# Decay attention: the key bias as two rows of the second score product, the causal mask as an addend of the minimum

## The chip, the cores and the metric

The kernel runs on one core of one Trainium2 chip. The metric is the device time of one execution in microseconds (us), and the time of a kernel is the median of several runs. Beside the runs, one execution is taken by the hardware profiler; every duration that is quoted comes from such an execution.

The engines' names in the profile: PE is TensorE's matrix products, PEld its weight loads, DVE is VectorE, ACT is ScalarE, POOL is GpSimd and SP the engine that issues most loads. "L733" is line 733 of the kernel.

## The reference

The kernel computes one layer of a hybrid trunk on 1024 frames of 1024 features: a state-space branch and a forgetting-attention branch side by side, then cross-attention into 256 memory tokens, then a gated FFN. The change touches the forgetting attention alone, 8 heads of 64:

```python
def forgetting_attention(q, k, v, f_logit):
    scale = 1.0 / math.sqrt(hd)
    cum_log_f = jnp.cumsum(jax.nn.log_sigmoid(f_logit.astype(jnp.float32)), axis=1)
    ...
        s = jnp.einsum('bqhd,bkhd->bhqk', qb, kb).astype(jnp.float32) * scale
        bias = cum_log_f[:, :, q0:k_end, None] - cum_log_f[:, :, None, :k_end]
        ...
        s = jnp.where(mask, s + bias, NEG_INF)
        p = jax.nn.softmax(s, axis=-1)
        outs.append(jnp.einsum('bhqk,bkhd->bqhd', p.astype(v.dtype), vb))
```

A query sees the keys up to its own position. The bias has one part for the query and one for the key. The query's part is the same for all keys of a row, so the softmax does not see it, and the kernel uses the key's part only.

## The kernel before

**Number format.** The large products run in a rounded 32-bit format (F32R). Where full precision is wanted, an operand is split into a rounded high part and the low remainder: `split` (L112) has ACT copy the high part (L113) and VectorE subtract it (L115, or L117 with a factor). `mm3` (L121) is then three products: high x high, high x low, low x high (L122 to L124).

**Stages.** (1) The input projections, with the state-space branch's coefficients worked out on VectorE beside them. `qk_tile` (L284) makes a block of q or k, takes it out of PSUM on VectorE (L289), splits it (through L113 and L115) and has POOL's queue store both halves in `qk_d` (L297, L298). q is stored with the factor -0.125, so all that follows works with negated scores, and the softmax's maximum is a minimum. In the middle of this stage `f_gate` (L336) turns the gate's logits, takes the logarithm of the sigmoid and its running sum over the 1024 frames (L348) in a tile of 8 rows, one per head, and POOL's queue stores that in `nc_d` (L349). The state-space branch then ends on VectorE (L621 to L624); SP loads its matrix T (L632), and `ssm_out` multiplies with it (L643, L644). (2) The attention stage, `fox` (L705), with fillers beside it. (3) The output projection, cross-attention and FFN, nearly all of it products on PE.

**The attention stage.** `fox` goes through 64 units, a head h and a block t of 128 queries, head by head. For each unit there are three steps, and their instructions are offered in a pipeline: the scores of a unit come two units ahead of its turning.

- `prepare(h)` (L709), offered at block 1 of the head before, issues five loads on SP's queue: the head's row of `nc_d`, broadcast to all 128 rows (`ncb`, a tile of tag b, 2 buffers, L714); q's high rows above q's low rows (`qs`, tag a, L718); and into `ka` k's high and low rows, twice, in rows 0 to 63 and 64 to 127 (L720).
- `scores(h, t)` (L722) fills a PSUM tile `s` (two buffers) with (t + 1) x 128 columns, at most 512 in one product: first `qs` against k's high rows, then `qs` against k's low rows (L730, L731). So each product sums over 128 rows: 64 with q's high part and 64 with its low part. A third, bf16 product of the identity with `maskb` adds 1e30 to the diagonal block's keys that lie ahead of the query (L733). Then one VectorE operation adds `ncb`, writes the sums to the tile `c` and leaves each row's minimum (L737, with a second instruction that reads the accumulator). ACT takes the exponential with the minimum as its bias and sums it (L739), VectorE takes the reciprocal (L740) and scales (L741).
- `turn(h, t)` (L744) transposes the unit's blocks on PE (L758) and copies them out of PSUM on ACT or VectorE (L761, L763). After two units of two heads, `values` (L765) multiplies with v on halves of the array (L772, 64 columns each).

Fillers (L975) are offered beside this at a fixed rate (`paced`, L887): the second half of v (`v1`), the gated unit, the normalised memory (`mem_load`, VectorE's L959), the state-space half of the output projection, the memory's keys and values, and a product of weights for the cross-attention. They use the same four PSUM buffers `g`.

At the end of the stage the loads of stage 3 go into the buffers that the attention frees: t1 into tiles of tags a and b (L1039), the weights of the output projection (L1026).

**What sets the order.** The program is offered as written, but the order of the instructions on each engine is made by a planner: it simulates the kernel with its own costs, starts what is ready by priority, and gives buffers out as they come free. Each engine, and each queue of loads, then runs its list in that order, and an instruction that waits holds up what stands behind it on its engine.

Of the kernel before, what the change touches and what calls it, by code (L numbers as in the profile page):

```python
# [9 lines left out]
F32 = mybir.dt.float32  # L10
F32R = mybir.dt.float32r
BF16 = mybir.dt.bfloat16
AF = mybir.ActivationFunctionType
ALU = mybir.AluOpType
# [3 lines left out]
P = 128  # L18
S = 1024
# [5 lines left out]
NH = 8  # L25
# [27 lines left out]
def layer(ctx: ExitStack, tc: tile.TileContext, a, out):  # L53
# [30 lines left out]
    def sm(n, name):  # L84
        return small.tile([P, n], F32, name=name, tag=name)

    ident = const.tile([P, P], F32, name="ident")
    make_identity(nc, ident)
    identb = const.tile([P, P], BF16, name="identb")
    dve.tensor_copy(identb, ident)  # L90
    ones = const.tile([P, 1], F32, name="ones")
    dve.memset(ones, 1.0)
    epsc = const.tile([P, 2], F32, name="epsc")
    for i in range(2):
        dve.memset(epsc[:, i:i + 1], (EPS, 4 * EPS)[i])
    maskb = const.tile([P, P], BF16, name="maskb")
    pool.memset(maskb, 0.0)
    pool.affine_select(out=maskb, in_=maskb, pattern=[[-1, P]], compare_op=ALU.is_ge,
                       fill=-NEG, base=0, channel_multiplier=1)
    gains = const.tile([P, 5, KT], F32, name="gains")  # L100
    with tc.high_priority(offset=2 * 5000):
# [10 lines left out]
    def split(hi, lo, src, mul=None, lo_eng=None):  # L112
        first = act.activation(out=hi, in_=src, func=AF.Copy, scale=1.0 if mul is None else mul)  # L113
        if mul is None:
            (lo_eng or dve).tensor_tensor(out=lo, in0=src, in1=hi.bitcast(F32), op=ALU.subtract)  # L115
        else:
            dve.scalar_tensor_tensor(out=lo, in0=src, scalar=mul, in1=hi.bitcast(F32),  # L117
                                     op0=ALU.mult, op1=ALU.subtract)
        return first
# [29 lines left out]
    stA, stB, stC = pool, pool, pool  # L149
# [29 lines left out]
    v_d = dram.tile([NT, P, 512], F32, name="v_d")  # L179
    h_d = dram.tile([16, NG, HP + P], F32, name="h_d")  # L180
    T_d = dram.tile([2, P, 16 * P], F32, name="T_d")
    nc_d = dram.tile([NH, S], F32, name="nc_d")
    t1_d = dram.tile([L, NC, D], F32, name="t1_d")
    kv_d = dram.tile([16, P, 256], F32, name="kv_d")
    x1_d = dram.tile([NT, P, D], F32, name="x1_d")
# [9 lines left out]
    def tt(tag, shape=None, dt=F32):  # L195
        return t4.tile(shape or [P, S], dt, name=tag, tag=tag, bufs=BUFS[tag])

    def t2t(shape, dt=F32):
        return tt("t2", shape, dt)
# [136 lines left out]
    def f_gate(ftok):  # L336
        ps = s_ps([P, S])[0:NH]
        for j in range(NT):
            pe.transpose(ps[:, j * P:(j + 1) * P], ftok[:, j], ident)
        f, fl = ps, tt("a", [NH, S])  # L340
        dve.tensor_scalar(out=f, in0=ps, scalar1=fb, scalar2=None, op0=ALU.add)
        f = f.rearrange("p (j c) -> p c j", j=L)
        fc = fl.rearrange("p (c j) -> p c j", j=L)
        act.activation(out=fc, in_=f, func=AF.Abs)
        act.activation(out=fl, in_=fl, func=AF.Exp, scale=-1.0)
        act.activation(out=fl, in_=fl, func=AF.Ln, bias=1.0)
        dve.scalar_tensor_tensor(out=fc, in0=f, scalar=0.0, in1=fc, op0=ALU.min, op1=ALU.subtract)
        dve.tensor_tensor_scan(out=fl, data0=fl, data1=fl, initial=0.0, op0=ALU.add, op1=ALU.min)  # L348
        stA.dma_start(out=nc_d, in_=fl)  # L349


    def cmul(o_re, o_im, x_re, x_im, y_re, y_im, t):
# [352 lines left out]
    def fox(yf):  # L705
# [3 lines left out]
        def prepare(h):  # L709
            r0 = (h % 2) * 64  # L710
            qs = tt("a", [P, S], F32R)
            ka = slab([P, 2, S])
            ncb = tt("b")
            sp.dma_start(out=ncb, in_=nc_d[h:h + 1, :].broadcast_to([P, S]))  # L714
            heads[h] = (qs, ka, ncb)
            q, k = qs.bitcast(F32), ka.bitcast(F32)
            for t in range(2):
                sp.dma_start(out=q[t * 64:t * 64 + 64], in_=qk_d[h // 2, t, r0:r0 + 64])  # L718
            for rr in (0, 64):
                sp.dma_start(out=k[rr:rr + 64], in_=qk_d[4 + h // 2, :, r0:r0 + 64].rearrange("t p s -> p t s"))  # L720

        def scores(h, t):  # L722
            qs, ka, ncb = heads[h]
            ke = (t + 1) * P
            ps = s_ps([P, S])
            qt = qs[:, t * P:(t + 1) * P]
            for c0 in range(0, ke, 512):
                c1 = min(ke, c0 + 512)
                dg = c1 == ke
                pe.matmul(ps[:, c0:c1], qt, ka[:, 0, c0:c1], start=True, stop=False)  # L730
                pe.matmul(ps[:, c0:c1], qt, ka[:, 1, c0:c1], start=False, stop=not dg)  # L731
                if dg:
                    pe.matmul(ps[:, ke - P:ke], identb, maskb, start=False, stop=True)  # L733
            sc = tt("c")
            nlr = sm(3, "nlr")
            nm, l, rl = (nlr[:, i:i + 1] for i in range(3))
            dve.tensor_tensor_reduce(out=sc[:, :ke], in0=ps[:, :ke], in1=ncb[:, :ke], scale=1.0,  # L737
                                     scalar=3e38, op0=ALU.add, op1=ALU.min, accum_out=nm)
            last.append(act.activation(out=sc[:, :ke], in_=sc[:, :ke], func=AF.Exp, scale=-1.0, bias=nm, accum_out=l))  # L739
            dve.reciprocal(out=rl, in_=l)  # L740
            dve.tensor_scalar(out=sc[:, :ke], in0=sc[:, :ke], scalar1=rl, scalar2=None, op0=ALU.mult)  # L741
            units[h, t] = sc
# [873 lines left out]
```

## Time and profile before

| | us |
|---|---|
| median of 3 runs | 1416.56 |
| lowest and highest run | 1413.81, 1417.14 |
| the profiled execution | 1412.18 |
| its span, first to last instruction | 1410.4 |
| mean granted TensorE clock over the span | 0.990 |

| products on PE in the attention stage | number | mean of one, ns |
|---|---|---|
| score products of 512 columns, L730 and L731 | 48 and 48 | 449 and 405 |
| mask products, L733 | 64 | 233 |
| transpositions, L758 | 288 | 280 |
| value products of 256 columns, L772 | 256 | 395 |

How to read it: the span is what the profiler saw between the first and the last instruction; the execution's own time has a little around it. Products are pipelined, so one's duration is longer than the time until the next starts: what a product costs is read from the starts. "Granted clock" is the share of TensorE's full speed that it was allowed in a stretch.

### The profile page before, as it was taken

To read this page: it belongs to the slowest core of one execution; us is meant where nothing else is said; L and a number is where in the kernel's file an instruction comes from. 1 tells how busy PE (TensorE), PEld (TensorE's weight loads), DVE (VectorE), ACT (ScalarE), POOL (GpSimd) and SP (SyncE) were. 2 spreads that over 40 slices of the span, in tenths; PEclk is the share of its full clock that TensorE was granted. 3 is DMA by queue.
4 is the path that set the end of the run, shared out by engine and by line. 5 is a ranking of instruction groups with operands and counts; after the bars stand their busy time and mean duration, and the time that the engine had idled before them with its cause. 6 is when DMAs were issued, how large, how long until landed. Compare 5 with 4: busy or idle time off the path is not lost.

```text
span 1410.4 us, 20272 instructions
## 1 busy us (share of the span) xinstructions
PE 1381.5 (98%) x7353; PEld 1163.3 (82%) x7353; DVE 952.1 (68%) x1719; ACT 652.8 (46%) x1289; POOL 378.7 (27%) x430
## 2 busy tenths in 40 slices
PE   9999999999999898999999999999999999999997
PEld 7889888889888786888888788888888888888886
DVE  8949945857666687545467767777776676555566
ACT  7383345666566555433344532333333334544351
POOL 0011110011111133001021377676766651000021
PEclk9999999889999999999999999999999999999999
DMA  6335665357562855024467345554444447965544
GB/s 217 91 107 162 204 224 135 91 165 224 187 180 95 214 185 201 1 83 159 147 213 250 102 174 195 186 173 168 144 159 151 162 150 244 344 203 194 179 165 164
DMA packets 104502, 239.45 MB, mean 170 GB/s; under 512 B 11465, under 2 KB 40137, under 8 KB 104273
## 3 DMA queue, kind: packets, MB, share of 16 engines
q1 hardware_dynamic: 85872, 176.24, 39.8%
q0 software_dynamic: 18528, 61.91, 12.3%
q8 instruction: 58, 0.95, 0.3%
q14 instruction: 44, 0.35, 0.1%
HBM read 169.43 MB, written 77.33 MB: 175 GB/s over the span
## 4 chain that ended last, share of the span: by engine, by line
PE 60%; DVE 1%; ACT 0%; issue 0%; DVEq 0%; ACTq 0%
PE x L1281 17%; PE g L1281 13%; PE x L1544 7%; PE g L1544 7%; PE x L123 2%; PE x L124 2%; PE g L122 2%; PE x L122 2%; PE g L124 2%; PE g L123 2%; PE g L1066 1%; PE g L1177 1%; DVE c L1054 0%; DVE whl L115 0%; ACT yt L1048 0%
## 5 line engine op out<-in xcount | busy, mean ns | idle before, releaser
L1281 PE MATMUL x<-slab,op 128*128 128x512 f32 x984 | 233.2, 389 | 0.5 <-DVE op L115 0.5
L1281 PEld LDWEIGHTS x<-slab,op 128*128 128x128 f32 x984 | 184.7, 188 | 39.2 <-DVE op L115 1.0
L1281 PE MATMUL g<-slab,op 128*128 128x512 f32 x744 | 178.7, 389 | 0.0
L115 DVE TENSOR_TENSOR slab<-slab 128x1024 fp32r<-128x1024 f32 (+2 forms) x92 | 110.6, 1208 | 86.6 <-ACT slab L113 84.4
L1281 PEld LDWEIGHTS g<-slab,op 128*128 128x128 f32 x744 | 139.7, 188 | 29.0
L122 PE MATMUL g<-slab,whl 128*128 128x512 f32 (+1 forms) x416 | 151.7, 365 | 0.8 <-ACT slab L485 0.4
L124 PE MATMUL g<-slab,whl 128*128 128x512 f32 (+1 forms) x416 | 148.9, 359 | 0.0
L123 PE MATMUL g<-slab,whl 128*128 128x512 f32 (+1 forms) x416 | 148.3, 356 | 0.0
L113 ACT ACTIVATE slab<-slab 128x1024 fp32r<-128x1024 f32 (+2 forms) x92 | 94.9, 1036 | 107.9 <-DMA slab<-hs_d 79.0
L1544 PE MATMUL g<-slab 128*128 128x512 f32 x462 | 126.6, 389 | 0.0
L1544 PE MATMUL x<-slab 128*128 128x512 f32 x462 | 126.6, 389 | 0.0
L1544 PEld LDWEIGHTS g<-slab 128*128 128x128 f32 x462 | 86.7, 188 | 18.0
L1544 PEld LDWEIGHTS x<-slab 128*128 128x128 f32 x462 | 86.7, 188 | 18.0
L115 DVE TENSOR_TENSOR op<-slab,op 128x512 fp32r<-128x512 f32 x80 | 84.4, 1066 | 11.6 <-ACT op L113 11.3
L1357 POOL TENSOR_TENSOR wt<-wt 128x256 f32<-128x256 f32 x88 | 83.0, 943 | 21.3 <-DMA wt<-in_w_down 18.0
L122 PEld LDWEIGHTS g<-slab,whl 128*128 128x128 f32 x416 | 78.6, 189 | 12.0 <-ACT whl L113 0.6
L124 PEld LDWEIGHTS g<-slab,whl 128*128 128x128 f32 x416 | 78.4, 189 | 11.7 <-DVE whl L115 0.2
L122 PE MATMUL g<-whl,slab 128*128 128x256 f32 (+2 forms) x288 | 86.8, 310 | 1.2 <-ACT yt L318 0.7
L123 PEld LDWEIGHTS g<-slab,whl 128*128 128x128 f32 x416 | 78.6, 189 | 10.8
L113 ACT ACTIVATE op<-slab 128x512 fp32r<-128x512 f32 x80 | 50.0, 627 | 79.3 <-PE x L1281 38.0
L124 PE MATMUL g<-whl,slab 128*128 128x256 f32 (+2 forms) x288 | 85.9, 299 | 0.0
L123 PE MATMUL g<-whl,slab 128*128 128x256 f32 (+2 forms) x288 | 85.9, 298 | 0.0
(385 smaller groups left out, 2890.6 us busy)
## 6 DMA issues: line engine op xcount, KB each, us to landing
hs_d<-ev POOLq DMA_DIRECT2D x77, 256.0 KB, 2.6
slab<-hs_d SPq DMA_DIRECT2D x35, 512.0 KB
wt<-in_w_down SPq DMA_DIRECT2D x44, 256.0 KB
wt_d<-wt POOLq DMA_DIRECT2D x22, 512.0 KB, 5.1
slab<-in_w_gate SPq DMA_DIRECT2D x20, 512.0 KB
slab<-in_w_up SPq DMA_DIRECT2D x20, 512.0 KB
slab<-wt_d SPq DMA_DIRECT2D x20, 512.0 KB
wd_d<-in_w_down SPq DMA_DIRECT2D x33, 256.0 KB
```

What stands on the lines that cost most here:

```text
L113: first = act.activation(out=hi, in_=src, func=AF.Copy, scale=1.0 if mul is None else mul)
L115: (lo_eng or dve).tensor_tensor(out=lo, in0=src, in1=hi.bitcast(F32), op=ALU.subtract)
L122: pe.matmul(ps, lh, rh, start=first, stop=False)
L123: pe.matmul(ps, lh, rl, start=False, stop=False)
L124: pe.matmul(ps, ll, rh, start=False, stop=last)
L1066: pe.transpose(tp[:, k], src[:, (k0 + k) * P:(k0 + k + 1) * P], ident)
L1177: turned = pe.transpose(tp[:, k], h3[:, (4 * n + k) * P:(4 * n + k + 1) * P], ident)
L1281: pe.matmul(ps, x[:, k], y[:, k], start=first and k + n == 0, stop=k == 3 and n == 2, skip_group_check=not first)
L1357: pool.tensor_tensor(out=o, in0=x, in1=y, op=ALU.subtract)
L1544: pe.matmul(banks[n][j], xo[:, u, js], wo[:, v], start=ends[0] and k == 0, stop=ends[1] and k == 2, skip_group_check=onto is not None)
```

## The change

The key's bias leaves VectorE's addition and enters through the second score product. Its low-part sum is cut from 128 rows to 66: 64 rows of q's high part against k's low part, and two rows of ones (`one_d`) against the bias, split into a rounded high row and a low row. (q's low part against k's low part is no longer computed.) For that `f_gate` splits the running sum in two halves of 512 columns, stores a high and a low row per head, and fills and stores the rows of ones. `prepare` builds a second tile `q1` of 66 rows in place of `ncb`, and `ka` gets the bias in rows 64 and 65 of its low half.

VectorE's addition then has its second operand free, and it takes the mask: a constant of 512 columns, zero but for its last 128. The diagonal block is always the last 128 columns of a row, so the operation takes the constant's last columns. For blocks 4 to 7 the row is longer than 512, and the operation is made twice: on the first 512 columns, with one zero column repeated as the addend, and on the rest, starting from the first one's minimum (`low`). The product with the identity (L733) and the identity in bf16 go.

```diff
-    identb = const.tile([P, P], BF16, name="identb")
-    dve.tensor_copy(identb, ident)
...
-    maskb = const.tile([P, P], BF16, name="maskb")
+    maskb = const.tile([P, 512], BF16, name="maskb")
     pool.memset(maskb, 0.0)
-    pool.affine_select(out=maskb, in_=maskb, pattern=[[-1, P]], compare_op=ALU.is_ge,
+    pool.affine_select(out=maskb[:, 384:], in_=maskb[:, 384:], pattern=[[-1, P]], compare_op=ALU.is_ge,
                        fill=-NEG, base=0, channel_multiplier=1)
...
-    nc_d = dram.tile([NH, S], F32, name="nc_d")
+    nc_d = dram.tile([NH, 2, S], F32, name="nc_d")
+    one_d = dram.tile([2, S], F32, name="one_d")
...
         dve.tensor_tensor_scan(out=fl, data0=fl, data1=fl, initial=0.0, op0=ALU.add, op1=ALU.min)
-        stA.dma_start(out=nc_d, in_=fl)
+        for h in range(2):
+            hs = slice(h * 512, h * 512 + 512)
+            hi = t2t([NH, 512], F32R)
+            split(hi, fl.bitcast(F32R)[:, hs], fl[:, hs])
+            stA.dma_start(out=nc_d[:, 0, hs], in_=hi.bitcast(F32))
+        stA.dma_start(out=nc_d[:, 1], in_=fl)
+        one = tt("yt", [2, 256])
+        dve.memset(one, 1.0)
+        for i in range(4):
+            stA.dma_start(out=one_d[:, i * 256:i * 256 + 256], in_=one)
...
             ka = slab([P, 2, S])
-            ncb = tt("b")
-            sp.dma_start(out=ncb, in_=nc_d[h:h + 1, :].broadcast_to([P, S]))
-            heads[h] = (qs, ka, ncb)
-            q, k = qs.bitcast(F32), ka.bitcast(F32)
+            q1 = tt("b", [66, S], F32R)
+            heads[h] = (qs, q1, ka)
+            q, k, o = qs.bitcast(F32), ka.bitcast(F32), q1.bitcast(F32)
             for t in range(2):
                 sp.dma_start(out=q[t * 64:t * 64 + 64], in_=qk_d[h // 2, t, r0:r0 + 64])
-            for rr in (0, 64):
-                sp.dma_start(out=k[rr:rr + 64], in_=qk_d[4 + h // 2, :, r0:r0 + 64].rearrange("t p s -> p t s"))
+            sp.dma_start(out=k[0:64], in_=qk_d[4 + h // 2, :, r0:r0 + 64].rearrange("t p s -> p t s"))
+            sp.dma_start(out=k[64:128, 0], in_=qk_d[4 + h // 2, 0, r0:r0 + 64])
+            sp.dma_start(out=o[0:64], in_=qk_d[h // 2, 0, r0:r0 + 64])
+            sp.dma_start(out=o[64:66], in_=one_d)
+            sp.dma_start(out=k[64:66, 1], in_=nc_d[h])
...
             for c0 in range(0, ke, 512):
                 c1 = min(ke, c0 + 512)
-                dg = c1 == ke
-                pe.matmul(ps[:, c0:c1], qt, ka[:, 0, c0:c1], start=True, stop=False)
-                pe.matmul(ps[:, c0:c1], qt, ka[:, 1, c0:c1], start=False, stop=not dg)
-                if dg:
-                    pe.matmul(ps[:, ke - P:ke], identb, maskb, start=False, stop=True)
-            sc = tt("c")
-            nlr = sm(3, "nlr")
-            nm, l, rl = (nlr[:, i:i + 1] for i in range(3))
-            dve.tensor_tensor_reduce(out=sc[:, :ke], in0=ps[:, :ke], in1=ncb[:, :ke], scale=1.0,
-                                     scalar=3e38, op0=ALU.add, op1=ALU.min, accum_out=nm)
+                pe.matmul(ps[:, c0:c1], qs[:, ts], ka[:, 0, c0:c1], start=True, stop=False)
+                pe.matmul(ps[:, c0:c1], q1[:, ts], ka[0:66, 1, c0:c1], start=False, stop=True)
+                add = maskb[:, 512 - (c1 - c0):] if c1 == ke else maskb[:, 0:1].broadcast_to([P, 512])
+                dve.tensor_tensor_reduce(out=sc[:, c0:c1], in0=ps[:, c0:c1], in1=add, scale=1.0,
+                                         scalar=low if c0 else 3e38, op0=ALU.add, op1=ALU.min,
+                                         accum_out=nm if c1 == ke else low)
```

More of the change, by code (lines that the diff above doesn't have):

```diff
@@ L722, in scores @@
+            sp.dma_start(out=k[64:128, 0], in_=qk_d[4 + h // 2, 0, r0:r0 + 64])
+            sp.dma_start(out=o[0:64], in_=qk_d[h // 2, 0, r0:r0 + 64])
+            sp.dma_start(out=o[64:66], in_=one_d)
+            sp.dma_start(out=k[64:66, 1], in_=nc_d[h])
         def scores(h, t):
-            qs, ka, ncb = heads[h]
+            qs, q1, ka = heads[h]
             ke = (t + 1) * P
             ps = s_ps([P, S])
-            qt = qs[:, t * P:(t + 1) * P]
+            ts = slice(t * P, (t + 1) * P)
@@ L727, in scores @@
+            sc = tt("c")
+            nlr = sm(4, "nlr")
+            nm, l, rl, low = (nlr[:, i:i + 1] for i in range(4))
             for c0 in range(0, ke, 512):
                 c1 = min(ke, c0 + 512)
-                dg = c1 == ke
-                pe.matmul(ps[:, c0:c1], qt, ka[:, 0, c0:c1], start=True, stop=False)
-                pe.matmul(ps[:, c0:c1], qt, ka[:, 1, c0:c1], start=False, stop=not dg)
-                if dg:
-                    pe.matmul(ps[:, ke - P:ke], identb, maskb, start=False, stop=True)
```

## The prediction

> **What bounds the kernel now.** I read the page first, then the table by stage, then PE's timeline inside the attention stage.
>
> ```profile
> span 1410.4 us, 20272 instructions
> PE 1381.5 (98%) x7353; PEld 1163.3 (82%) x7353; DVE 952.1 (68%) x1719; ACT 652.8 (46%) x1289; POOL 378.7 (27%) x430
> PE 60%; DVE 1%; ACT 0%; issue 0%; DVEq 0%; ACTq 0%
> ```
>
> The span is TensorE's: it is busy 98% of it, and of the part of the last-ending chain that is named, PE has 60% and the others together 1%. So a product that is taken out counts where PE is back to back, and an added VectorE operation counts only where PE waits for VectorE. Which of the two holds is read by stage:
>
> ```profile
> core 0: us, PE busy (x) PEld busy (x) DVE busy (x) ACT busy (x) POOL busy (x), PEclk, DMA share, GB/s
> 154.00:190.00 36.00, 35.04 (x172) 29.58 (x172) 35.90 (x59) 16.26 (x27) 6.23 (x12) 1.00 0.62 193
> 228.00:270.00 42.00, 40.54 (x235) 33.57 (x233) 35.68 (x84) 30.87 (x68) 0.54 (x1) 1.00 0.41 102
> 270.00:290.00 20.00, 15.54 (x72) 12.88 (x74) 14.59 (x36) 14.60 (x31) 1.31 (x2) 0.57 0.39 111
> 320.00:462.00 142.00, 142.00 (x1156) 127.49 (x1154) 97.29 (x230) 88.71 (x193) 23.41 (x34) 1.00 0.59 171
> 462.00:490.00 28.00, 24.40 (x179) 18.90 (x178) 17.10 (x29) 15.33 (x29) 2.59 (x2) 1.00 0.81 219
> ```
>
> From 320 to 462 PE never stops (142.00 of 142.00) and VectorE has 45 us to spare: there the change is worth what it saves on PE. Three places are different: 154 to 190, where VectorE has no idle time at all; 270 to 290, where PE waits and its granted clock falls to 0.57; and 462 to 490, where the stage drains.
>
> **The 64 mask products that go (L733).**
>
> ```profile
> L733 PE MATMUL s<-maskb,identb x64: 229/230/330, 228.7 to 459.0; 128*128 128x128 bf16 x64
> ```
> ```profile
> 330.55 0.22 PE L730 MATMUL s<-slab,a 128*128 128x128 f32 x1
> 330.62 0.28 PE L731 MATMUL s<-slab,a 128*128 128x128 f32 x1
> 330.73 0.23 PE L733 MATMUL s<-maskb,identb 128*128 128x128 bf16 x1
> 330.80 0.61 PE L758 MATMUL g<-ident,c 128*128 128x128 f32 x4
> ...
> 331.93 0.28 PE L731 MATMUL s<-slab,a 128*128 128x256 f32 x1
> 332.05 0.23 PE L733 MATMUL s<-maskb,identb 128*128 128x128 bf16 x1
> 332.09 0.36 PE L124 MATMUL g<-slab,whl 128*128 128x256 f32 x1
> 332.30 0.28 PE L122 MATMUL g<-slab,whl 128*128 128x256 f32 x1
> 332.41 0.28 PE L123 MATMUL g<-slab,whl 128*128 128x256 f32 x1
> ```
>
> A mask product's 0.23 us is not its price, since products overlap; the price is what it does to the starts around it. Before a transposition, the next start comes 0.07 later (330.73 to 330.80). Before another product it comes only 0.04 later, but the step behind that is 0.21 instead of 0.11: from 331.93 to 332.41 there are 0.48 us where three undisturbed steps would take 0.35 to 0.36, so 0.12. Followed along PE's timeline from 228.7 to 459.0, 34 of the 64 stand before a transposition and 30 before something else: 34 x 0.07 + 30 x 0.12 = 2.4 + 3.6 = 6.0 us. The upper bound adds 0.04 for the 16 whose last score product is 128 wide (the step 330.62 to 330.73 is 0.11, the one before it 0.07): 6.6. The lower bound lets the transpositions cost the same without a mask ahead of them: 3.6. I take 6.0.
>
> **The second product, now 66 rows deep.** Each L731 stays one product of the same columns: 96 before and after. No row of this trace has a product with fewer than 128 rows, so its cost is bounded by the nearest: nothing, as for the other 128*128 products, or a change of array shape, as the value products show (a rival below). I take nothing, since it still fills 128 columns and more than half the rows. The Trainium skill ("TensorE: Matmul & The Clock Gate", on LDWEIGHTS) says the same of the weight load: its length follows the columns, not the rows; no run here shows it yet.
>
> **The minimum, split in two for blocks 4 to 7.**
>
> ```profile
> L737 DVE CUSTOM_DVE_ANT_0 c<-s,b 128x1024 f32<-128x1024 f32 x8 | 9.8, 1219 | 0.3 <-PE s L733 0.3
> L737 DVE CUSTOM_DVE_ANT_0 c<-s,b 128x640 f32<-128x640 f32 x8 | 6.6, 821 | 4.3 <-PE s L733 4.2
> L737 DVE CUSTOM_DVE_ANT_0 c<-s,b 128x512 f32<-128x512 f32 x8 | 5.5, 688 | 2.5 <-PE g L758 1.4 <-PE s L733 1.2
> L737 DVE DVE_READ_ACCUMULATOR2_ANT nlr<- 128x1 f32 x64 | 5.3, 84 | 0.0
> L737 DVE CUSTOM_DVE_ANT_0 c<-s,b 128x128 f32<-128x128 f32 x8 | 2.3, 286 | 3.7 <-PE g L758 3.1 <-PE s L733 0.6
> ```
>
> Two of 512 are 2 x 688 = 1376 against 1219, and 512 + 128 are 974 against 821: 0.155 us more either way, and one more read of the accumulator, 0.084. That is 0.24 a unit, 32 units, 7.7 us on VectorE. The second piece starts from the first one's result; a hand-over of 0 to 0.1 us each is not in any row of this kind, and makes it 7.7 to 10.9. That the addend is now bf16, and for the first piece one column repeated, I take as free: the operation handles about one element per ns (688 - 286 = 402 ns for 384 columns), whatever feeds it; a gain from the narrower operand is not excluded, and would be below nothing. Behind VectorE's longer unit wait ACT's exponential, the reciprocal and scaling, and PE's transpositions two units later. From 290 to 462 PE has other products queued all the time and VectorE's spare 45 us cover the 6 to 9 us that fall there: nothing. The Trainium skill ("VectorE: DVE Perf Modes", "The DRAIN you can't avoid") speaks against this part of the change: a per-row statistic used as the next operation's scalar needs a wait between the two, and it advises fewer operations; by that the hand-over is a real wait at the upper end of the bound, and the sum stays as it is.
>
> In head 0 the cover is missing:
>
> ```profile
> 270.64 1.76 DVE L959 TENSOR_TENSOR raw<-raw,t 128x256 f32<-128x256 f32 x5
> 272.31 0.95 DVE L737 CUSTOM_DVE_ANT_0 c<-s,b 128x768 f32<-128x768 f32 x1
> ```
> ```profile
> 273.33 0.80 PE L730 MATMUL s<-slab,a 128*128 128x512 f32 x1 [2.00 <-DVE nlr L737]
> ```
>
> PE stands 2.00 us until block 5's minimum frees its score tile. Two split units (blocks 4 and 5) lie ahead of that release: 2 x 0.24 = 0.5 us later. And the masks that are gone before it only bring PE to this wait sooner. L733 alone in the same stretch (PE and PEld busy, instructions in brackets):
>
> ```profile
> 228.00:270.00 42.00, 3.46 (x15) 1.44 (x15) 1.00 0.41 102
> ```
>
> Fifteen of the 64, at 0.1 each 1.5 us, of which between nothing and all is lost. VectorE itself had short waits for PE before it, so I take half, 0.7.
>
> **The gate (f_gate).** Added: two copies on ACT, two subtractions and a small fill on VectorE, six DMA issues more on POOL. The rows of the same two operations of 512 columns, and of the one issue that was there:
>
> ```profile
> L113 ACT ACTIVATE t<-a x8: 612/616/633, 153.9 to 188.7; 128x512 fp32r<-128x512 f32 x8
> L115 DVE TENSOR_TENSOR a<-a,t x8: 671/681/689, 157.3 to 190.7; 128x512 fp32r<-128x512 f32 x8
> ```
> ```profile
> L349 POOL DMA_DIRECT2D nc_d<-a x1: 522/522/522, 156.2 to 156.2; - x1
> ```
> ```profile
> 181.82 1.08 DVE L624 TENSOR_TENSOR b<-b,slab 128x896 f32<-128x896 f32 x1
> ```
> ```profile
> 182.94 1.13 SPq L632 DMA_DIRECT2D slab<-T_d  x2
> ```
> ```profile
> 188.77 0.46 PE L643 MATMUL g<-slab 128*128 128x128 f32 x2 [0.96 <-DMA slab<-T_d]
> ```
>
> ACT (1.2 us) and POOL (6 x 0.52 = 3.1 us, with the qk_d stores of L297 and L298 queued behind) have idle time for it: 16.26 and 6.23 busy of 36. VectorE has none, so 2 x 0.68 = 1.4 us, up to 2.0 with the fill, pass along its queue: L624 ends later, the load of T (L632) goes out later, and PE's wait of 0.96 at L643 grows by as much, unless the planner puts a block of v1's products in front, of which there are plenty. Bounds 0 to 2.0; I take 0.5, nearer to nothing, because PE's list in this stage is laid out anew from the same costs.
>
> **Loads of a head (prepare).** Seven issues instead of five on SP, all short. Of 2.0 MB, the broadcast (0.5) and one low half of k (0.25) go, and q's high rows (0.25) come again: 1.5 MB, less traffic than before. PE is covered from 290 on. One release moves: the tile of tag b was freed by the minimum, now by the last score product.
>
> ```profile
> 461.94 1.22 DVE L737 CUSTOM_DVE_ANT_0 c<-s,b 128x1024 f32<-128x1024 f32 x1
> ```
> ```profile
> 463.19 1.19 SPq L1039 DMA_DIRECT2D b<-t_d  x2
> ```
> ```profile
> 477.08 0.73 PE L122 MATMUL x<-slab 128*128 128x512 f32 x2 [1.55 <-ACT slab L113]
> ```
>
> At the end of the stage SP's load into b goes out as the last minimum ends, and the weights queued behind it reach PE 1.55 us late. The last mask stood at 459.0, so the release comes some 4 us sooner; the gain is 0 to 1.55, and with DMA at 0.81 I take half, 0.7. Nothing else moves; the mask's wider constant and the cast that goes lie in the first two microseconds.
>
> **Sum:** -6.0 + 0.7 + 0.5 + 0.5 - 0.7 = -5.0 us. The profiled execution took 1412.18, its span and 1.8 around it, and would take 1407.2. The median of the runs is 1416.56, 4.4 above it; the same 5.0 less is **1411.6 us**. Bounds of the terms together: -8.2 to +0.6.
>
> **Rivals.**
> *The half-clock spell of head 0 goes.* From 270 to 290 the granted clock is 0.57: 0.43 x 20 = 8.6 us lost. It begins with the wait of 2.00. For: the plan is made anew, and a few products of other work at this place would fill the wait. Against: VectorE's load here grows. 1411.6 - 8.6 = 1403.0.
> *A second spell, at L643 (slower).* Waits of 0.96 and 1.55 left the clock at 1.00, the one of 2.00 did not, so it decides between. If all of f_gate's 1.4 to 2.0 us reach L643, its wait is 2.4 to 3.0: 1411.6 - 0.5 + 1.4 + 8.6 = 1421.1. For: VectorE is full there and this chain already ends last. Against: v1's products can go in front.
> *The saving comes back as waits.* The order on every engine is a planner's, from its own costs; with 64 products fewer and 32 minima more it lays out fillers and heads differently, and waits like those of head 0 come elsewhere: 1412.5 to 1418, middle 1415.
> *Sixty-six rows count as another array shape.*
>
> ```profile
> 306.89 0.28 PE L124 MATMUL g<-slab,whl 128*128 128x256 f32 x1
> 307.10 3.46 PE L772 MATMUL g<-slab 128*64 128x256 f32 x32
> ```
>
> Into the 128*64 value products the step is 0.21 instead of 0.12. Were each second product entered and left so: 96 x 2 x 0.09 = 17 us, 1428.9; the change would not do what it says. The Trainium skill ("TensorEngine Tiling (Array Packing)", Key Properties) has it that a change of tiling mode drains the array; its list has row modes of 64 and 32 only, which speaks for 66 rows staying in the full one.
>
> **Chances.** Forecast 0.54, spell gone 0.10, saving swallowed 0.22, second spell 0.10, array shape 0.04. About 0.3% (4.2 us, below 1412.3) is what a measurement can tell from no change. Of the forecast's 0.54, 0.40 lies below that and 0.14 within; of the swallowed 0.22, 0.19 within and 0.03 above. Faster 0.40 + 0.10 = 0.50; same 0.14 + 0.19 = 0.33; slower 0.03 + 0.10 + 0.04 = 0.17. The range goes from the spell gone, 1403, to 1419, past the swallowed case; the second spell and the array shape lie outside. The forecast's own range is 1408 to 1415.
>
> **What the profile after would show.** Right: no L733; PE's steps from second product to the next unchanged by the 66 rows; 96 minima whose pairs add 0.24 us or a little more; PE without idle from 290 to 460; the last score product some 6 us earlier relative to the first. Wrong: a step of 0.2 behind each second product; PE waits for VectorE beyond head 0; a wait at L643 over 2 us; another stretch with the clock under 1.00, or none.

## The result, and the profile after

After takes 1419.51 us (median of 10 runs, 1417.14 to 1423.60), before 1414.37 on the same chip (10 runs, 1411.56 to 1417.14): a ratio of 1.0040, 95% interval 1.0028 to 1.0052. The change costs 5.1 us where 5 less were forecast. (The forecast started from a median of three runs, 1416.56; with the ten runs' 1414.37 the same step leads to 1409.4, further still from what came.) The profiled execution of after took 1417.77, its span 5.6 us more than before's:

```profile
span 1416.0 us, 20272 instructions
PE 1380.0 (97%) x7289; PEld 1161.3 (82%) x7289; DVE 957.1 (68%) x1785; ACT 651.9 (46%) x1291; POOL 381.6 (27%) x436
```

The 64 mask products are gone (7353 less 64 is 7289) and PE is busy 1.5 us less, in a span that is 5.6 longer: PE is idle 7 us more. The table by stage, same stretches as in the prediction and one more, says where (busy time of PE, PEld, DVE, ACT, POOL, then the clock, the DMA share and GB/s):

```profile
154.00:190.00 36.00, 34.38 (x168) 28.99 (x166) 35.02 (x60) 17.20 (x28) 6.90 (x13) 1.00 0.58 183
228.00:270.00 42.00, 39.98 (x212) 33.23 (x211) 34.20 (x87) 29.96 (x64) 1.08 (x2) 0.96 0.35 85
270.00:290.00 20.00, 17.66 (x107) 14.91 (x106) 15.82 (x47) 14.22 (x31) 1.45 (x2) 0.74 0.20 54
320.00:462.00 142.00, 140.47 (x1106) 125.31 (x1106) 100.26 (x272) 88.81 (x195) 23.33 (x34) 1.00 0.56 158
462.00:490.00 28.00, 24.52 (x173) 19.01 (x169) 16.71 (x30) 13.63 (x25) 2.48 (x2) 1.00 0.71 206
490.00:530.00 40.00, 34.20 (x187) 30.06 (x188) 27.11 (x50) 20.71 (x63) 12.04 (x11) 0.91 0.54 162
```

Before's row for the added stretch:

```profile
490.00:530.00 40.00, 39.41 (x218) 34.42 (x219) 30.72 (x58) 22.19 (x71) 14.28 (x13) 1.00 0.61 195
```

Behind the attention, where the change touches nothing, PE is busy 5.2 us less and runs part of the time at a lower clock. In the full stretch, 320 to 462, PE now has gaps: 1.5 us. The waits of PE in after, longest groups (us in total, times, longest):

```profile
PE g L236 <- POOL d L795: 4.6, 1, 4.6
PE s L742 <- DVE nlr L745: 3.4, 6, 1.4
PE g L651 <- DMA slab<-T_d: 2.5, 1, 2.5
...
PE g L767 <- DVE c L750: 1.7, 3, 0.9
```

The first is new: the attention's token sums (each token's sum of squares over the features, for a normalisation) wait for POOL. The second was 3.5 us in 3 waits in before. The third was 0.96. The fourth, transpositions that wait for VectorE's scaling, is new.

Read from PE's timeline, the execution up to its last product falls into four parts (some 7.6 us follow in either kernel):

| us | before | after | difference |
|---|---|---|---|
| A: start to first score product | 228.6 | 229.6 | +1.0 |
| B: to last value product | 257.4 | 254.6 | -2.9 |
| C: to last product of the output projection | 85.8 | 93.3 | +7.5 |
| D: to the last product of all | 830.9 | 830.9 | 0.0 |

So B kept half of the masks' saving, and C, behind the attention, lost more than all of it. Part of both is the clock. PE ran at half speed for 17.1 us of B and 6.8 of C in before, for 13.7 and 10.2 in after; at most half of such a time is lost, so the clock took up to 1.7 us less in B and up to 1.7 more in C. Without it B would be about 1.2 shorter and C about 5.8 longer. In B itself the products do what was expected. Two units, of two and of three blocks, in PE's timeline of after:

```profile
332.36 0.28 PE L742 MATMUL s<-slab,a 128*128 128x256 f32 x1
332.48 0.28 PE L743 MATMUL s<-slab,b 66*128 66x256 f32 x1
332.60 0.34 PE L742 MATMUL s<-slab,a 128*128 128x384 f32 x1
332.77 0.34 PE L743 MATMUL s<-slab,b 66*128 66x384 f32 x1
332.95 1.04 PE L767 MATMUL g<-ident,c 128*128 128x128 f32 x8
```

From the 66-row product to the next there are 0.12 and 0.18 us, from the 128-row product ahead of it 0.12 and 0.17: the depth costs nothing, and no step of 0.2 shows as at another array shape. The weight loads agree (mean 196 ns for 66 rows, 194 for 128), as the Trainium skill says in "TensorE: Matmul & The Clock Gate", section on LDWEIGHTS: their length follows the columns.

The groups of the minimum in after (busy us, mean ns, idle before):

```profile
L745 DVE CUSTOM_DVE_ANT_0 c<-s,maskb 128x512 f32<-128x512 f32 x40 | 27.5, 688 | 12.2 <-PE s L743 6.5 <-PE g L767 4.8
L745 DVE DVE_READ_ACCUMULATOR2_ANT nlr<- 128x1 f32 x96 | 7.9, 82 | 0.0
L745 DVE CUSTOM_DVE_ANT_0 c<-s,maskb,nlr 128x512 f32<-128x512 f32 x8 | 6.0, 744 | 2.6 <-PE s L743 2.6
```

For 1024 columns that is 688 + 744 + 82 = 1514 ns against 1219 and no second read: 0.295 a unit, inside the 0.24 to 0.34 of the prediction. A second piece takes 56 ns longer than a first of the same size. The mask as its addend is not the reason: the 40 of the first line include block 3's, which read the mask too, and none of the 40 takes more than 693 ns. So it goes with the start value that the first piece hands over. The Trainium skill ("VectorE: DVE Perf Modes", "The DRAIN you can't avoid") has it that a per-row result can be read stale by the very next operation unless a wait or another operation stands between. Whether the 56 ns are such a wait no run here shows.

### The profile page after: what moved, and what is told of

Its sections match the earlier page's. It is cut to its first block, busy times and chain, and to the rows that moved or that the text cites. A ratio compares the mean times of both kernels' runs of the same rounds, so it can differ in the third digit from the quotient of the medians.

```text
span 1416.0 us, 20272 instructions
## 1 busy us (share of the span) xinstructions
PE 1380.0 (97%) x7289; PEld 1161.3 (82%) x7289; DVE 957.1 (68%) x1785; ACT 651.9 (46%) x1291; POOL 381.6 (27%) x436
## 4 chain that ended last, share of the span: by engine, by line
PE 60%; DVE 1%; ACT 0%; issue 0%; DVEq 0%; ACTq 0%
PE x L1290 17%; PE g L1290 13%; PE x L1553 7%; PE g L1553 7%; PE x L121 2%; PE x L122 2%; PE g L120 2%; PE x L120 2%; PE g L122 2%; PE g L121 2%; PE g L1075 1%; PE g L1186 1%; DVE c L1063 0%; DVE whl L113 0%; ACT yt L1057 0%
## 5 line engine op out<-in xcount | busy, mean ns | idle before, releaser
L1290 PEld LDWEIGHTS x<-slab,op 128*128 128x128 f32 x984 | 184.6, 188 | 39.3 <-DVE op L113 1.0
```

The lines of the kernel that those rows point to most:

```text
L1290: pe.matmul(ps, x[:, k], y[:, k], start=first and k + n == 0, stop=k == 3 and n == 2, skip_group_check=not first)
```

## The experiments

Each kernel ran in five rounds beside the kernel before on the same chip; the chips' medians of before lie between 1414.0 and 1416.6, so ratios are compared. A difference of two kernels is given in % of before (0.1% is 1.4 us); from the intervals, such a difference is uncertain by some 0.2. Of each kernel there is one trace, while its runs spread by up to 0.7% (e2_gate_pool: 1413.62 to 1423.78), so the ratios decide and the traces show where. The clock column is the mean granted clock of the kernel's runs, and behind the stroke that of the runs of before beside it. In e4_no_mask, e9_one_min and e30_one_min_fl the causal mask inside the diagonal blocks is left out.

| kernel | median us | ratio to before, 95% | clock | store of the sum holds L288 | token sums wait for POOL |
|---|---|---|---|---|---|
| before | 1414.4 | 1 | 0.9907 | 0 | 0 |
| e8_before_rate100 | 1417.37 | 1.0018 (1.0004 to 1.0032) | 0.9899 / 0.9911 | 0 | 4.3 |
| e4_no_mask | 1406.98 | 0.9950 (0.9930 to 0.9969) | 0.9910 / 0.9908 | 0.9 | 0 |
| e5_before_split | 1410.84 | 0.9973 (0.9962 to 0.9983) | 0.9946 / 0.9907 | 0 | 3.3 |
| e23_before_split_square | 1409.36 | 0.9944 (0.9928 to 0.9959) | 0.9940 / 0.9905 | 0 | 0 |
| after | 1419.51 | 1.0040 (1.0028 to 1.0052) | 0.9888 | 0.9 | 4.6 |
| e8_after_rate100 | 1424.67 | 1.0064 (1.0046 to 1.0082) | 0.9880 / 0.9907 | 2.0 | 0 |
| e8_after_rate105 | 1416.01 | 1.0010 (0.9996 to 1.0024) | 0.9886 / 0.9911 | 2.1 | 0 |
| e1_square_first | 1417.77 | 1.0023 (1.0013 to 1.0033) | 0.9896 / 0.9908 | 2.0 | 0.2 |
| e2_gate_pool | 1418.65 | 1.0032 (1.0018 to 1.0046) | 0.9895 / 0.9908 | order moved | 4.7 |
| e7_square_gate | 1419.91 | 1.0032 (1.0019 to 1.0046) | 0.9888 / 0.9908 | order moved | 0.2 |
| e16_rows_only | 1418.35 | 1.0026 (1.0013 to 1.0040) | 0.9891 / 0.9911 | 1.4 | 0 |
| e9_one_min | 1411.76 | 0.9978 (0.9964 to 0.9991) | 0.9905 / 0.9907 | 1.2 | 0 |
| e30_one_min_fl | 1408.71 | 0.9958 (0.9946 to 0.9971) | 0.9912 / 0.9901 | 0 | 0 |
| e10_wide_mask | 1418.37 | 1.0027 (1.0011 to 1.0044) | 0.9828 / 0.9907 | 0 | 0 |
| e14_half_split | 1414.35 | 0.9997 (0.9983 to 1.0011) | 0.9884 / 0.9911 | 0.9 | 4.7 |
| e20_fl_apart | 1417.05 | 1.0010 (0.9994 to 1.0025) | 0.9894 / 0.9905 | 0 | 1.7 |
| e26_after_fixed | 1414.87 | 0.9985 (0.9974 to 0.9997) | 0.9912 / 0.9905 | 0 | 0 |
| e29_fixed_less_dve | 1414.23 | 0.9999 (0.9989 to 1.0009) | 0.9912 / 0.9901 | 0 | 0.2 |
| e21_half_split_fixed | 1406.37 | 0.9933 (0.9917 to 0.9949) | 0.9908 / 0.9905 | 0 | 0 |

**The clock of the runs.** A step of 0.001 in the clock is 1.4 us of work at full speed. In the 130 runs of before, the 13 at 0.988 or less took 1418.2 on average, the 17 at 0.993 or more 1412.5: about 1.0 us for 0.001. So after's 0.9888 against 0.9907 is an estimated 2 us of its 5.1, and e5's 0.9946 is an estimated 4 us, all that it gained. (One of e10's runs is listed at 0.936 and was no slower than the others, so a single run's figure can be off; the other nine average 0.9880.) No kernel was built to hold the clock still, and a wait can bring it down, so what follows names it wherever it carries a result.

**First: the wait of the token sums, the gate, the masks.** The reason for the new wait stands in ACT's timeline. In after:

```profile
496.21 1.06 ACT L111 ACTIVATE whl<-raw 128x1024 fp32r<-128x1024 f32 x1 [4.70 <-DMA raw<-in_wqT]
497.17 0.37 ACT L794 ACTIVATE yt<-g 128x256 f32<-128x256 f32 x1
```

and in before:

```profile
492.28 0.38 ACT L785 ACTIVATE yt<-g 128x256 f32<-128x256 f32 x1 [1.38 <-DVE slab L117]
495.04 1.06 ACT L113 ACTIVATE whl<-raw 128x1024 fp32r<-128x1024 f32 x1 [2.37 <-DMA raw<-in_wqT]
```

The last square of the attention (L794, was L785), which POOL and then the token sums need, stands next to a split of a weight in ACT's list, and that weight is still being loaded. In before the square goes first; in after the split does, and holds it up while it waits 4.70 us for its load. e1 turns the two round:

```diff
-                act.activation(out=sq, in_=yp, func=AF.Square)
+                sq_at.append(act.activation(out=sq, in_=yp, func=AF.Square))
...
-            wq = [load_w(a["wqT"][2 * hd + d], P) for d in range(2)]
+            with ExitStack() as stack:
+                if (c, h) == (1, 1):
+                    stack.enter_context(tc.issue_after(sq_at[-1].ins))
+                wq = [load_w(a["wqT"][2 * hd + d], P) for d in range(2)]
```

> The changed kernel; only the split of one later weight (wqT) on ACT is told to stand behind the last square of the attention's sums. Theory (order): that split waits for its load with the square stuck behind it, PE waits 4.6 us for the sums and then runs at half clock for a while; without it the kernel takes about 1412.5, 7 us less than the changed one. Rival (loads): the end of the attention stage is set by the weights' loads through two buffers, whatever stands where on ACT; the last split was 1.2 us later than in the kernel before, so about 1415.5. Rival (longer minimum): the 32 added VectorE operations are the cost; 1419.5, no change.

The wait went (0.2 left) and the time fell by 0.17%, 2.4 us, not 7: in the traces PE waited longer for VectorE in the output projection (3.0 us against 1.5), and A ended 2.1 us later (first score product at 231.7): the first state-space product waited 3.4 us for its load, and 3.4 us at half clock followed, which after has not. e2 has POOL make the gate's subtractions (`split(..., lo_eng=pool)` at L351), e7 is both.

> The changed kernel with the gate's two subtractions on POOL instead of VectorE. Theory (order): PE's wait for T at the state-space product falls from 2.5 us to about 1.0 as before the change, everything until 490 us lies 1.5 us earlier, but the square still stands behind the split: 1418. Rival (loads): what is won ahead of 470 us is swallowed at the loads, 1419.5. Rival (longer minimum): 1419.5.

> Both edits, the square first and the gate's subtractions on POOL. Theory (order): 1419.5 - 7 - 1.5 = 1411. Rival (loads): 1415.5, as with the square first alone. Rival (longer minimum): 1419.5.

Neither helped: the first state-space product waited 3.6 and 3.7 us for its load, longer than in after. So the time of VectorE's two subtractions was not the cause. e4 is the kernel before without L733:

> The kernel before without its 64 mask products and nothing else changed: the causal mask inside the diagonal blocks is left out. It prices the removed part alone. Theory (order): PE comes 5 to 6 us earlier to the end of the attention (460 us) and the kernel takes 1409 if no new wait comes with the new plan. Rival (loads): PE comes as early to 460 us, but leaves the stage no earlier, 1414.

7.3 us less, at the same clock as before: the masks' price was about right, and it reaches the end. So the change's other parts cost some 12 us.

**Second: which part.** e5 gives the kernel before the split minimum, adding `ncb[:, c0:c1]`; e9 gives after one minimum with `maskb[:, 0:1].broadcast_to([P, ke])` as the addend; e10 makes the mask 1024 columns wide, in the front's tiles, with `"yt": 1`; e8_after_rate100 sets `RATE = 1.00`.

> The kernel before with one part of the change alone: its minimum over key columns goes in pieces of 512 (two for query tiles 4 to 7, chained through the column low), still adding the key bias; its mask products stay. Theory S (the second piece of the minimum is what costs: VectorE ends each late unit some 0.3 us later and TensorE meets it): about 6 us over before, 1420, with TensorE waiting for VectorE's minimum or scaling after the first head as in after. Theory N (what comes before the attention, the gate's longer chain and the loads, is what costs): within 1.5 us of before, 1413 to 1416. Theory M (the order that the planner writes out lands differently in each kernel, and that alone moves the end): anywhere from 1410 to 1420, without waits for the minimum.

> After with the minimum as one operation over all key columns, its addend one zero column repeated; the causal mask inside the diagonal blocks is left out, so that its time is that of the change without the split. Theory S: the 5 us come back and the masks' price of 7 shows, 1407 to 1411. Theory N: as after, 1417 to 1420, the wait of the first state-space product for its load as long as in after (2.5 us against 0.96). Theory M: anywhere between.

> After with the mask constant 1024 columns wide, so that the minimum is one operation over all key columns and the mask still enters; the constant lies with the front's tiles and the small tile yt has one buffer instead of two to make room. Theory S: as e9_one_min, 1407 to 1412, and below the kernel before. Theory N: as after, 1417 to 1420. If the second yt buffer mattered, over e9_one_min by what the token sums' squares then wait (some 1 to 2 us).

> After with the filler's pace set to 1.00 instead of 1.02, nothing else: the written-out order of fillers among the attention's units shifts a little, and no operation is added or taken away. Theory M: a move of 2 us or more either way. Theories S and N: within 1.5 us of after, 1418 to 1421.

Theory S, 6 us over before, fell: with the same second pieces the kernel before became 0.27% faster. That they help is not shown, since the clock can make the whole gain: in e5's trace the half-clock spell of head 0 lasts 3.4 us instead of 17.1, which alone can be worth 6.8. (The prediction's rival "the half-clock spell of head 0 goes" nearly came true here, in another kernel.) So did N alone: e9 keeps the gate, the rows and the loads and, with no masks, is faster than before. M's sign is in the pace: 1.00 for 1.02 costs after 0.24%. e10 tells little of the mask, since its one buffer of yt cost 7 us in A (its first score product came at 236.0). PE's row for it:

```profile
PE g L120 <- ACT yt L317: 7.4, 1, 7.4
```

e16 puts the masks back into e9. e14 reads the first half of the addend of blocks 4 and 5 from the zero columns of the same constant, so that only blocks 6 and 7 need two pieces:

```diff
+            cut = 512 if ke > 768 else 0
...
+                w = n // 2
+                add = bass.AP(add.tensor, maskb[:, 384 - w:].offset, [list(add.ap[0]), [P, 2], [1, w]])
```

> After with the mask products of before put back and the minimum as one operation (its addend a zero column repeated): the change's key-bias rows, with the gate's longer chain and the new loads, and nothing else of it. Theory F (the rows' feed costs about 5 us: the pair without masks and without the split, 1411.8 with the rows against 1407.0 without, differs by that): 1418 to 1420. Theory M (the order that the planner writes out is drawn anew by any edit and moves the end by some 5 us either way): no value is excluded between 1409 and 1420; near before, 1413 to 1416, would speak against F.

> After with 16 second pieces of the minimum instead of 32: for query tiles 4 and 5 the addend's first half is read from the zero columns of the same 512-column constant, so one operation does the row; tiles 6 and 7 keep two. All of the change's arithmetic stays. If the split costs in proportion to its number (theory S, from e9_one_min 1411.8 and after 1419.5): 1415 to 1417. Theory M: anywhere between 1409 and 1422, and not in line with the number of pieces.

> The kernel before with the filler's pace at 1.00 instead of 1.02, no operation added or taken away. Theory M: over 1.5 us away from 1414.2, either way (after moved by 5 us with this edit). If M is wrong for before: 1413 to 1415.5.

> After with the filler's pace at 1.05, no operation added or taken away. Theory M: over 1.5 us away from 1419.5, either way; one such order of the changed kernel may lie below before. If the 5 us are a price of the changed operations themselves: 1417 to 1422.

The masks and the rows now add up in two pairs each: without masks -0.50% (e4 to before) and -0.48% (e9 to e16); with the rows +0.26% (e16 to before) and +0.28% (e9 to e4), 4 us. That the pairs agree so well is in part chance: e16 ran at 0.9891 against 0.9911, an estimated 2 us, while e4 and e9 ran within 0.0002 of before. Clear of the clock, by the same estimate, the masks are 5 to 7 us and the rows 2 to 4. And the pace alone, no operation added, moves after by 0.54% from 1.00 to 1.05. At pace 1.00 the kernel before has the wait of the token sums too, as has e5:

```profile
PE g L237 <- POOL d L786: 4.3, 1, 4.3
```

```profile
PE g L237 <- POOL d L789: 3.3, 1, 3.3
```

So that wait is no price of the rows, the mask or the second pieces. It comes with the written order, which before drew well and after badly.

**Third: where the rows' price lies.** VectorE's timeline in after has a wait where before has none, at L288, which takes a block of q or k out of PSUM (idle time in brackets):

```profile
162.92 1.13 DVE L288 SCALAR_TENSOR_TENSOR a<-g,d 128x512 f32<-128x512 f32 x1 [0.87 <-DMA nc_d<-a]
```

In before the same operation ran at 159.18, early among the steps of the state-space chain, and waited for nothing:

```profile
159.18 1.12 DVE L289 SCALAR_TENSOR_TENSOR a<-g,d 128x512 f32<-128x512 f32 x1
```

It writes a tile of tag a, of which there are two, and the gate's running sum is in one of them. The sum used to be stored at once; now it is held through two copies and two subtractions, and its own store stands behind two others on POOL's queue. Either L288 waits, or the planner puts it off, and in both cases it and its followers come among the chain's steps on a VectorE that is busy 35.0 of 36 us. The chain's four steps of L632 (L624 in before) all come later, the third at 184.6 instead of 181.8, the last at 192.1 instead of 188.0; the first load of T goes out at 186.3 instead of 182.9, and PE's first state-space product starts at 190.9 instead of 188.8. The rows are not needed for this wait: e4, the kernel before without its masks, has it too (0.9), with the sum stored at once: where the planner puts L289 counts as well. e2 shows it from the other side: POOL's subtractions take 1.8 us each, the tile is held longer, and L288 stands at 166.92. e20 moves the sum to a tile that nobody wants at this time:

```diff
-        f, fl = ps, tt("a", [NH, S])
+        f, fl = ps, tt("e", [NH, S])
```

> After with the gate's running sum in the tile of tag e instead of one of the two of tag a, nothing else. Theory W1: in after, VectorE's taking of a block of q or k out of PSUM (L288) waits 0.9 us for the store of the running sum out of its tile (0.9 to 2.1 us in seven of the nine kernels with the rows, none in three of the four without), and the state-space chain behind it on VectorE's queue ends 4 us later than in before. Then here the wait is gone, the last step of that chain starts at 188 to 190 us instead of 192.1, the first state-space product starts about 189 instead of 190.9, and the time is 1.5 to 3 below after: 1416.5 to 1418. If the wait is only the place where another lateness shows: no change, 1419 to 1420, the chain as late as before.

> The changed kernel with 16 second pieces of the minimum (e14_half_split, 1414.35), its running sum in the tile of tag e, and the last split of wqT told to stand behind the last square, as in e1_square_first. All of the change's arithmetic stays. If the two waits are worth their length (2 and 4.8 us): 1407 to 1409, below the kernel before. If the second is worth what e1_square_first gave (1.7): 1410 to 1411.5. If neither: 1414.

> The kernel before with its minimum in two pieces (e5_before_split, 1410.84) and the last split of wqT told to stand behind the last square; no other instruction moves by more than a few places. In e5's profile the token sums waited 3.3 us for POOL's last sum, as in after. Theory W2 (the wait is a place in ACT's written order, not a price of the change, and it reaches the end): the wait is gone and the time is 2 to 5 below e5's: 1406 to 1409. If the wait only moves on to the output projection: 1410 to 1411.5.

> After with both repairs: the running sum in the tile of tag e, and the last split of wqT behind the last square. Theory W1 with W2: about what the two singles give together, 2 and 1.7 to 4.8 below after: 1412.5 to 1416. If what is left is the price of the second pieces of the minimum on VectorE, the time stays 3 us and more above e21_half_split_fixed, and TensorE's waits for the minimum and the scaling inside the attention are the difference.

In e20 L288 runs at 159.66 and waits for nothing, as in before; PE's row for the state-space product is

```profile
PE g L651 <- DVE b L631: 1.6, 1, 1.6
```

The time fell by 0.30%. PE's list is the same in both kernels, instruction for instruction, so this is no new draw of its order. The chain's end moved by less than expected, to 191.3, and the first state-space product to 190.26: in the profiles A is 0.9 us shorter. The wait of the token sums is 2.9 shorter as well (1.7 for 4.6), and the clock is an estimated 1 us of the gain, so the 0.30% are not the tile's alone. e23 took the wait of the token sums out of e5, with no other instruction moved by more than a few places, and gained 0.29%, 4 us, as W2 says, at nearly the same clock (0.9940 and 0.9946). e26, with both repairs, is 0.15% below before, where after was 0.40% above. e21, with both repairs and 16 second pieces, is the fastest: 0.9933 of before, 9.5 us.

**Fourth: what is left.** e29 takes 18 copies from VectorE (`h > 4` for `h > 1` at L769) in e26; e30 has e20's tile in e9.

> e26_after_fixed (32 second pieces, both repairs) with 18 of VectorE's 36 copies of transposed blocks given to ACT (those of heads 2 to 4), some 18 x 0.53 = 9.6 us of VectorE's work, about what the second pieces add to it inside the attention (168.3 us against 159.1 in before); the order on every engine changes only where they stood. Theory V (what is left of the second pieces' price is VectorE's lateness, which TensorE meets): TensorE's waits for the minimum and the scaling (3.4 and 2.0 us in e26) shrink, and the time goes from 1414.9 towards e21_half_split_fixed's 1406.4, 3 us and more below e26. Theory M (the rest is the written order): within 2 us of e26. If ACT becomes late in its place: over e26.

> e9_one_min (the rows, one minimum per unit, the causal mask inside the diagonal blocks left out) with the running sum in the tile of tag e; the order on every engine changes only around the gate. Theory W1: the wait for the store (1.2 us there) goes, and the time is 2 to 4 below e9's ratio of 0.9978, at 0.995 to 0.9965 of before; the rows then cost at most 2 us over e4_no_mask (0.995). If the rows' price lies elsewhere: 0.9975 to 0.9985.

The stretch 229 to 463 in e26 and then in e29:

```profile
229.00:463.00 234.00, 227.60 (x1663) 199.88 (x1662) 168.35 (x445) 149.84 (x328) 28.06 (x42) 0.97 0.50 139
```

```profile
229.00:463.00 234.00, 227.52 (x1676) 200.34 (x1674) 162.80 (x432) 157.94 (x351) 28.20 (x42) 0.98 0.51 141
```

VectorE has 5.6 us less to do in it, PE is as busy as in e26, and the waits for the minimum are no shorter (3.9 us in e29 against 3.4); the ratio is within 0.15% of e26's. So VectorE's load in sum is not what the second pieces cost. That a single minimum ends later is not excluded, since those waits stayed. e30 gained 0.20% on e9, with PE's list the same; about half of that is the clock (0.9912 against 0.9905, beside 0.9901 and 0.9907 in before). With one minimum the rows cost 0.08% over e4_no_mask, nothing that can be told, and e4 has the wait at L289 that e30 has not. So the gate's tile is a part of the rows' price, 1 to 3 us; that it is most of it is not shown.

## Why the prediction was wrong

The forecast was a sum of local prices, and most of these were about right. **The masks**, -6.0, bounds 3.6 to 6.6: 7.3 measured (e4), 6.8 in the other pair, of which an estimated 2 are the clock. **The 66 rows**, nothing: right by the starts above, and the rival with another array shape is out. **The second pieces**, 0.24 to 0.34 us each on VectorE: 0.295.

Four steps failed.

*Loads of a head: "I take half, 0.7. Nothing else moves".* For the end of the attention a gain of 0.7 was forecast; part C lost 7.5, up to 1.7 of them to the clock. A wait of 4.6 us arose there through an order on ACT that the change does not name, and it is worth 0.17 to 0.29% (after to e1, e20 to e26, e5 to e23): 2.4 to 4.1 us. The prediction knew that a planner writes the order, and had "the saving comes back as waits" as a rival with 0.22, 1412.5 to 1418. The kind was right, the chance and the size too small; the result lies just outside the range, which reached 1419, past this rival.

*The gate, "bounds 0 to 2.0; I take 0.5".* With the sum in another tile the time fell by 0.20% (e9 to e30) and 0.30% (after to e20), 3 to 4 us; without the clock and the shorter wait of the token sums 1 to 3 are left. The mechanism was another. The prediction costed what the gate's new instructions take on each engine. It did not ask how long they hold the tile that they read, and who waits for that tile. The store's 0.52 us stood in its rows; L289, which writes the same tag, and that tag's two buffers stood in the kernel.

*"From 290 to 462 PE has other products queued all the time ...: nothing."* PE has gaps of 1.5 us between 320 and 462, waits for the minimum and the scaling beyond head 0, which the prediction named as a sign of being wrong. Gaps of 1.5 to 1.6 us stand in all of after, e20, e26 and e29, with 32 second pieces; none in e14 and e21 with 16 (320 to 450), and none in e16 and e30 with one minimum (e9's 0.9 us is a wait for another). But e23, with 32 pieces and without the rows, has none either (320 to 455). What the second pieces cost in the end is **not settled**. Alone in the kernel before they measured -0.27%, which the clock can make alone, and in after, against e9, +0.62%, of which the wait of the token sums and an estimated 2 us of clock are parts. Where neither of the two waits stands, 32 of them are at +0.27% over none (e26 to e30) and 16 at -0.25% (e21 to e30), and the clock does not make that: e26, e30 and e21 lead before by 0.0007, 0.0011 and 0.0003 in it. No price of an operation has both signs; e29 speaks against VectorE's load in sum; the written order, which alone makes 0.54% (the pace), is the likely cause, but no run held it fixed while the pieces were added.

*Head 0, +0.7 and +0.5, and the clock.* The long spell there got shorter (270 to 290 at 0.74 instead of 0.57) and a new one came at 233. Added up in windows of 2 us from 180 to 580, (1 - granted clock) x 2 gives 11.9 us lost in before and 11.9 in after: in these two executions the clock moved and cost the same. Over the runs it did not: 0.9888 against 0.9907 is an estimated 2 us, a term that the sum put at nothing. The rival "a second spell at L643" set its point between waits of 1.55 and 2.00; the wait grew to 2.54 and the clock stayed. In e1, e2 and e7, where it grew to 3.4 and more, a spell did come there, of 3.4 us. After's row:

```profile
186.00:200.00 14.00, 10.82 (x90) 10.29 (x90) 7.15 (x8) 7.39 (x10) 2.68 (x5) 1.00 0.93 320
```

The sum in place of the forecast, in % of before: masks -0.5, rows +0.27, of which the gate's tile is a part, the end's wait about +0.25, which makes +0.02. The 0.38 up to the measured 0.40 are the second pieces together with the order that came with them. Each of these figures is a difference of whole kernels, uncertain by 0.2 and with its share of clock, so the sum shows where the time went and is no set of prices.

## What to carry to other kernels

When an instruction is added, price the buffer that it keeps as well as the engine that it uses: find the next writer of that tag, its engine, and what stands behind it on a full engine. Where a planner writes the order, a small edit draws a new one, and a neutral change of pace shows how far such draws lie apart (0.5% here); a forecast needs that as its width, and a result of that size needs single-edit kernels, and a look at the granted clock of their runs, before it is put down to an operation. Look at the last consumers of a stage first: an instruction that others need, behind one that waits for a load, is a cheap repair (2.4 to 4.1 us here; with both repairs and half of the second pieces the changed kernel stands 9.5 us below before).

## What the runs showed of the hardware

The half-clock spells come in pieces. Four windows around the wait of the token sums in after:

```profile
496.00:498.00 2.00, 0.00 (x0) 0.00 (x0) 0.70 (x1) 1.69 (x3) 0.39 (x1) 0.60 0.05 18
498.00:500.00 2.00, 0.84 (x4) 0.84 (x5) 0.92 (x2) 0.47 (x1) 1.10 (x1) 0.50 0.38 41
500.00:502.00 2.00, 2.00 (x6) 1.71 (x7) 1.51 (x7) 1.21 (x4) 0.00 (x0) 0.50 0.67 256
502.00:504.00 2.00, 2.00 (x11) 1.71 (x11) 1.97 (x5) 0.13 (x1) 0.00 (x0) 0.69 0.64 221
```

The loss is 2 x (0.40 + 0.50 + 0.50 + 0.31) = 3.42 us, a spell of 6.84 at half speed. The totals of the kernels are whole multiples of half of that, 1.71: 8.5 in e30 (5 times), 10.2 in e9 (6), 11.9 in before, after and e4 (7), 13.6 in e20 and e26 (8), 17.0 in e16 (10). A spell is thus a whole number of pieces of 3.41 us. The Trainium skill ("TensorE: Matmul & The Clock Gate", "What's actually happening") has a free-running window of 3413 ns, which agrees. It also has the clock fall after an idle window; here PE's wait of 2.00 us in head 0 of before was enough, and the 2.54 in front of L651 was not, so the length of a wait alone does not decide.

Where the wait lies does. In each of the 20 traces all spells start on one grid of 3.41 us. From 60 to 1390 us, 45 of the grid's windows at full clock had PE busy under 0.48, and each was followed by half clock; of 7534 at 0.70 or more none was; between the two it went either way (32 of 99). After's wait of 2.54 is shared by two windows, busy 0.75 and 0.50, and the clock stayed. A wait of 2.28 at the same place in e4 lies in one window, busy 0.33, and half clock followed. So a small shift of a wait against the grid can cost 1.7 us or save them, which is one way for one kernel's runs to differ.
